# Modulation columns of the SSD part loaded at the head of each pair into the two large "ex" buffers

## The chip, the cores and the metric

The kernel runs on one core of one Trainium2 chip. The metric is device time in microseconds (us); lower is better. TensorE (PE), VectorE (DVE), ScalarE (ACT), GpSimd (POOL) and the queue of loads and stores (SP) each run their own list of instructions in order, and wait for one another by semaphores.

## The reference

One decoder layer at sequence 1024 and width 1024, all in float32. The part that the change touches is the modulation: six sections of 1024 numbers, each a sum over the 1024 inputs.

```python
c_act = jax.nn.silu(c)
mod = jnp.einsum('bd,de->be', c_act, w_ada[l]) + b_ada[l]
sh1, sc1, g1, sh2, sc2, g2 = [m[:, None, :] for m in jnp.split(mod, 6, axis=-1)]
h = x * (1.0 + sc1) + sh1
y = hybrid_mixer(h, ...)            # SSD scan (16 heads) + attention (16 heads), then W_out
x = layer_norm(ALPHA * x + (1.0 + g1) * y, ln1_g[l], ln1_b[l])
h = x * (1.0 + sc2) + sh2
ff = square(relu(h @ w_ff_in)) @ w_ff_out
x = layer_norm(ALPHA * x + (1.0 + g2) * ff, ln2_g[l], ln2_b[l])
```

The first section pair (`sh1`, `sc1`) is needed before anything else. The others are needed only after the mixer, so the kernel spreads them over it.

## The kernel before

The kernel goes through a start (h is made, eight tiles `h_hl` of 128 rows), eight SSD head pairs, attention, the output projection and the MLP. A float32 operand is split into a high part and a low remainder (`split`: the high part on POOL, ACT or DVE, the remainder always by a DVE subtraction, line 85), and each product is three matmuls.

`w_ada` is laid out as 48 columns of 512 KB, `raw_ada`, 128 x 1024 numbers each. For most of them `ada_sum` loads the column (on SP), POOL multiplies it by `c_act` (line 132), and DVE reduces it to 128 x 128, `ada_red` (line 134). PE then sums over the partitions (`adar_ps`) and DVE adds the bias (`mod_t`, line 202). `ada_red` has four buffers (`bufs=4`).

`w_prep` loads 512 KB of a projection weight, `raw_w`, and splits it in two halves `w_hl` of 128 x 512. `raw_w` and the 14 `raw_ada` of the SSD part share one tag, "raw", with two buffers: a load of either waits until the last reader of the buffer's older content is done (the subtraction of a `w_hl`, or the reduction of a column).

The SSD pairs run in this loop; `ssd(p)` makes the decays (`ea` and `scores` on ACT, from rows that are read back from DRAM) and the state, `conv_tile` and `z_tile` make the projections of the next pair, and `ada_some(2)` starts two columns and ends the two of the pair before:

```python
for p in range(NPAIR - 1):
    wn = w_prep(w_in[XI + p + 1])[0]
    ssd(p, *xz[p])
    xz.append((conv_tile(p + 1, "qk", "qk", wn), z_tile(p + 1)))
    ...
    ada_some(2)
```

The tag "ex" has two buffers of 8 KB per partition. In the kernel before it is first used in attention, by `w2_sums`. What stands where on each engine is decided by a scheduler that lays the whole program out beforehand; the code above gives it the order in which things are asked for, and it may move an instruction ahead of others that its model holds to be late.

Of the kernel before, what the change touches and what calls it, by code (L numbers as in the profile page):

```python
# [32 lines left out]
def layer_kernel(ctx, tc, x, xT, cols, rows3, w_ada, b_ada, w_in, w_dtf, w_out, ln_rows, w1, w2, out):  # L33
    nc = tc.nc

    def tap(name, t):
        if TAPS is not None and name in TAPS:
            shape = list(t.shape)
            o = nc.dram_tensor(f"tap_{name}", shape, F32, kind="ExternalOutput").ap()
            nc.sync.dma_start(out=o, in_=t)  # L40
# [9 lines left out]
    def T4(tag, name, dt=F32, shape=(P, 1024)):  # L50
        return sb.tile(list(shape), dt, name=name, tag=tag, bufs=SLOTS[tag])

    def R4(tag, name, shape=(P, 1024)):
        return T4(tag, name, F32R, shape)
# [3 lines left out]
    def PT(tag, name, shape=(P, 512), dt=F32):  # L58
        return ps.tile(list(shape), dt, name=name, tag=tag, bufs=PB[tag])

    def mm(o, l, r, start, stop):
        nc.tensor.matmul(o, l, r, start=start, stop=stop)  # L62

    def load(o, i):
        return nc.sync.dma_start(out=o, in_=i)
# [29 lines left out]
    ones = cst.tile([P, P], F32, name="ones")  # L95
# [29 lines left out]
    SH1, SC1, G1, SH2, SC2, G2 = range(6)  # L125
    mod_t = cst.tile([P, 6, KT], F32, name="mod_t")

    def ada_sum(sec, j, tag, name):

        raw = T4(tag, "raw_ada", shape=(P, KT, P))  # L130
        load(raw, w_ada[sec * 8 + j])
        nc.gpsimd.tensor_tensor(raw, raw, c_act.unsqueeze(2).broadcast_to([P, KT, P]), op=ALU.mult)  # L132
        red = sb.tile([P, P], F32, name="ada_red", tag="q2", bufs=4)
        nc.vector.tensor_reduce(red, raw.rearrange("p k c -> p c k"), axis=mybir.AxisListType.X, op=ALU.add)  # L134
        return red
# [4 lines left out]
    ADA_TAGS = ["P"] * 5 + ["pt"] * 4 + ["cum"] * 2 + ["P"] * 5  # L140
# [4 lines left out]
    def h_tile(j):  # L145
        pst = PT("t", "ada_ps", (P, 2))
        for i, sec in enumerate((SC1, SH1)):
            if j < PE_ADA:
                raw = T4(ADA_TAGS[2 * j + i], "raw_ada", shape=(P, KT, P))
                load(raw, w_ada[sec * 8 + j])  # L150
                for k in range(KT):
                    mm(pst[:, i:i + 1], raw[:, k, :], c_act[:, k:k + 1], k == 0, k == KT - 1)
            else:
                mm(pst[:, i:i + 1], ada_sum(sec, j, ADA_TAGS[2 * j + i], "r"), ones[:, 0:1], True, True)
        nc.vector.scalar_tensor_tensor(mod_t[:, SC1, j:j + 1], pst[:, 0:1], 1.0, b_t[:, 8 + j:9 + j],
                                       op0=ALU.add, op1=ALU.add)
        nc.vector.tensor_tensor(mod_t[:, SH1, j:j + 1], pst[:, 1:2], b_t[:, j:j + 1], op=ALU.add)
        xt = T4("v", "xt")
        marks["xt"] = load(xt, xT[j * P:(j + 1) * P, :])
        nc.scalar.activation(xt, xt, AF.Identity, scale=mod_t[:, SC1, j:j + 1], bias=mod_t[:, SH1, j:j + 1])  # L160
        t = sb.tile([P, 2, T], F32R, name="h_hl", tag="hx", bufs=SLOTS["hx"])
        split(xt, t[:, 0, :], t[:, 1, :], "dve" if j >= HI_DVE else "act")
        hT.append((t[:, 0, :], t[:, 1, :]))
# [22 lines left out]
    g_rows = {}  # L186
    gsum = {}

    def ada_rest(sec, j):
        red = ada_sum(sec, j, "raw", "r")  # L190
        yield
        pst = PT("mm", "adar_ps", (P, P))
        if sec in (G1, G2):
            mm(pst, ones, red, True, True)
            if j == 0:
                gsum[sec] = dr.tile([P, 1024], F32, name=f"grow{sec}")
            g = sb.tile([P, P], F32, name="ada_g", tag="q2", bufs=4)
            nc.vector.tensor_copy(g, pst)
            load(gsum[sec][:, j * P:(j + 1) * P], g)
        else:  # L200
            mm(pst[:, 0:1], red, ones[:, 0:1], True, True)
            nc.vector.tensor_tensor(mod_t[:, sec, j:j + 1], pst[:, 0:1], b_t[:, sec * 8 + j:sec * 8 + j + 1], op=ALU.add)

    rest = [(s, j) for s in (SC2, SH2, G2, G1) for j in range(8)]

    pend = []

    def ada_some(n):
        for g in pend:
            next(g, None)  # L210
        pend.clear()
        for _ in range(min(n, len(rest))):
            g = ada_rest(*rest.pop(0))
            next(g)
            pend.append(g)


    def w_prep(src, hi_eng="pool", tag="w"):

        raw = T4("raw", "raw_w", shape=(P, KT, P))  # L220
        ld = load(raw, src)
        w = []
        for kh in range(2):
            t = R4(tag, "w_hl", (P, 2, 4, P))
            split(raw[:, kh * 4:kh * 4 + 4, :], t[:, 0], t[:, 1], hi_eng)
            w.append(t)
        return w, ld
# [4 lines left out]
    def proj(w, half, M=P, o=None, tag="mm", ks=range(KT)):  # L232
# [8 lines left out]
        return o  # L241

    h_tile(0)


# [6 lines left out]
    for j in range(1, KT):  # L252
        h_tile(j)
# [97 lines left out]
    def z_tile(i):  # L351
        w, _ = w_prep(w_in[ZI + i])
        z = T4("qk", "z_s")
        for half in range(2):
            o = proj(w, half, tag="t")
            nc.scalar.activation(z[:, half * 512:half * 512 + 512], o, AF.Silu)
        return z
# [24 lines left out]
    def ssd(p, xs, z):  # L382
        g = p // 4
        h0 = 2 * p
        xp = PT("S", "s2_ps", (P, 8, P))
        for b in range(8):
            nc.tensor.transpose(xp[:, b, :], xs[:, b * P:(b + 1) * P], identf)
        xc = T4("qk", "xc", shape=(P, 8, 2, 64))
        xd = T4("qk", "xd", shape=(P, 8, 2, 64))
        nc.vector.tensor_tensor(xc, xp.rearrange("p c (h d) -> p c h d", h=2),  # L390
                                dtn[:, :, h0:h0 + 2].unsqueeze(3).broadcast_to([P, 8, 2, 64]), op=ALU.mult)
        nc.gpsimd.tensor_tensor(xd, xc, dte[:, :, h0:h0 + 2].unsqueeze(3).broadcast_to([P, 8, 2, 64]), op=ALU.mult)

        stp = PT("S", "s2_ps", (P, 8, P))
        for b in range(7):
            mm(stp[:, b, :], BN[g][:, b, :], xd[:, b, :, :].rearrange("p h d -> p (h d)"), True, True)
        pv = T4("pt", "prev", shape=(P, 8, P))
        nc.vector.memset(pv[:, 0, :], 0.0)
        for b in range(7):
            for h in range(2):  # L400
                hs = slice(h * 64, h * 64 + 64)
                nc.vector.scalar_tensor_tensor(pv[:, b + 1, hs], pv[:, b, hs], etot[:, b, h0 + h:h0 + h + 1],
                                               stp[:, b, hs], op0=ALU.mult, op1=ALU.add)

        ea = T4("misc", "ea")
        for h in range(2):
            load(ea[h * 64:h * 64 + 64, :], rowd[h0 + h:h0 + h + 1, :].broadcast_to([64, T]))
        nc.scalar.activation(ea, ea, AF.Exp)

        ydg = PT("S", "s2_ps", (P, 8, P))  # L410
        scs = []
        for h in range(2):
            ar = T4("cum", "arow", shape=(P, 8, P))
            load(ar.rearrange("p c l -> p (c l)"), rowd[h0 + h:h0 + h + 1, :].broadcast_to([P, T]))
            sc = T4("v", "scores", shape=(P, 8, P))
            for b in range(8):
                nc.scalar.activation(sc[:, b, :], ar[:, b, :], AF.Relu, bias=cs[:, b, h0 + h:h0 + h + 1], scale=-1.0)  # L417
            nc.scalar.activation(sc, sc, AF.Exp, scale=-1.0)
            nc.vector.tensor_tensor(sc, sc, CBM[g], op=ALU.mult)
            scs.append(sc)  # L420
        for b in range(8):
            for h in range(2):
                mm(ydg[h * 64:h * 64 + 64, b, :], xc[:, b, h, :], scs[h][:, b, :], True, True)
        yo = PT("S", "s2_ps", (P, 8, P))
        for b in range(8):
            mm(yo[:, b, :], pv[:, b, :], CT[g][:, b * P:(b + 1) * P], True, True)
        nc.vector.tensor_tensor(ea, yo.rearrange("p c d -> p (c d)"), ea, op=ALU.mult)
        nc.vector.tensor_tensor(ea, ydg.rearrange("p c d -> p (c d)"), ea, op=ALU.add)
        nc.vector.scalar_tensor_tensor(ea, xs, dsk[:, p:p + 1], ea, op0=ALU.mult, op1=ALU.add)
        if p == 0:  # L430
            tap("ssdy0", ea)
        nc.vector.tensor_tensor(ea, ea, z, op=ALU.mult)
        store(yd[p], ea)
# [5 lines left out]
    xz = [(conv_tile(0, "qk", "qk", w_x), z_tile(0))]  # L439
    for p in range(NPAIR - 1):  # L440
        wn = w_prep(w_in[XI + p + 1])[0]
        ssd(p, *xz[p])
        xz.append((conv_tile(p + 1, "qk", "qk", wn), z_tile(p + 1)))
        if p == FR_AT:
            forget_rows()
        if p == 1:
            group_prep(1)
        ada_some(2)
# [798 lines left out]
```

## Time and profile before

| | |
|---|---|
| median of 3 runs | 1739.49 us (1738.86 to 1745.34) |
| profiled execution, its own time | 1744.44 us |
| its span, first to last instruction | 1742.7 us |
| PE busy | 1654.0 us, 95% |
| DVE busy | 1229.9 us, 71% |
| POOL busy | 821.6 us, 47% |
| ACT busy | 747.2 us, 43% |
| mean granted TensorE clock | 0.980 of full speed |

The span is divided by the program itself: the start is 0 to about 65 us, the SSD pairs reach to about 365 us, and the rest is attention, the output projection and the MLP. An engine is counted as busy while an instruction runs on it; "idle before" is the time in which it stood, and the name behind the arrow is what it waited for. TensorE's clock has two levels, 1.2 and 2.4 GHz, told here as a granted clock of 0.5 and 1.0 of full speed.

### The profile page before, as it was taken

What the parts mean: (1) busy time and instruction counts of PE and PEld (TensorE: products, weight loads), DVE (VectorE), ACT (ScalarE), POOL (GpSimd) and SP (SyncE); (2) the same over time, 40 slices, a digit from 0 to 9 for tenths busy, and PEclk for the clock granted to TensorE, in tenths of its full rate; (3) what the DMA queues carried; (4) which work ended last, traced back from release to release, by engine and by line L of the source; (5) the groups of instructions that cost most, each with busy time, mean ns of one, the idle gap of its engine ahead of it and who ended that gap; (6) DMA issues with size and microseconds to landing.
All of it is one profiled execution on the core that took longest, in us unless ns stands there. A gap on an engine that the chain in (4) does not pass through costs nothing.

```text
span 1742.7 us, 22932 instructions
## 1 busy us (share of the span) xinstructions
PE 1654.0 (95%) x8316; PEld 1368.7 (79%) x8316; DVE 1229.9 (71%) x1898; ACT 747.2 (43%) x1321; POOL 821.6 (47%) x670
## 2 busy tenths in 40 slices
PE   8989899899999999999899999799999999999996
PEld 6777787788877878888778887688888878888885
DVE  7755777686777777676665379986767855646668
ACT  3458355414444444444565334633332334343322
POOL 5121332256566466454442345566656624704535
PEclk9999999999999999999999999899999999999998
DMA  8134343334444534434324644043444596676512
GB/s 331 37 123 147 109 145 109 121 130 151 161 142 170 169 134 167 137 121 132 119 97 130 221 157 169 37 175 133 146 143 160 172 340 212 247 242 205 194 36 96
DMA packets 112032, 268.72 MB, mean 154 GB/s; under 512 B 10128, under 2 KB 37008, under 8 KB 111920
## 3 DMA queue, kind: packets, MB, share of 16 engines
q1 hardware_dynamic: 111920, 267.27, 44.2%
q8 instruction: 65, 1.06, 0.3%
q14 instruction: 47, 0.39, 0.1%
HBM read 194.22 MB, written 64.62 MB: 149 GB/s over the span
## 4 chain that ended last, share of the span: by engine, by line
PE 60%; DVE 15%; DMA 8%; ACT 7%; POOL 5%; issue 4%; SPq 0%; DVEq 0%; ACTq 0%; POOLq 0%
PE mm_ps L62 18%; PE f_ps L957 15%; PE s_ps L1073 9%; PE y_ps L1073 7%; PE s_ps L62 5%; PE o_ps L62 4%; DVE ada_red L134 3%; PE t_ps L546 3%; DMA w_b<-in_w_dram 2%; ACT scores L417 2%; POOL w_b L182 2%; DMA raw_ada<-in_w_ada_dram 1%; DVE w_hl L85 1%; DVE conv_a L346 1%; DVE h_hl L85 1%
## 5 line engine op out<-in xcount | busy, mean ns | idle before, releaser
L62 PE MATMUL mm_ps<-h_hl,w_hl 128*128 128x512 f32 x2016 | 504.5, 400 | 10.9 <-POOL w_hl L79 6.1
L62 PEld LDWEIGHTS mm_ps<-h_hl,w_hl 128*128 128x128 f32 x2016 | 373.5, 191 | 88.3 <-POOL w_hl L79 6.9
L85 DVE TENSOR_TENSOR w_op<-raw_w,w_op 128x512 fp32r<-128x512 f32 (+1 forms) x149 | 186.9, 1260 | 23.2 <-ACT w_op L81 22.6
L957 PE MATMUL f_ps<-h_s,w_op 128*128 128x512 f32 x768 | 183.8, 394 | 6.4 <-ACT h_s L81 3.3
L957 PEld LDWEIGHTS f_ps<-h_s,w_op 128*128 128x128 f32 x768 | 146.0, 190 | 38.4 <-ACT h_s L81 3.7
L524 POOL TENSOR_SCALAR probs<-probs,m 128x128 f32<-128x128 f32 (+7 forms) x128 | 104.5, 822 | 127.3 <-DVE m L523 122.8
L81 ACT CAST w_op<-raw_w 128x512 fp32r<-128x512 f32 (+1 forms) x149 | 114.5, 774 | 100.2 <-PE f_ps L957 53.0
L1073 PE MATMUL s_ps<-w_op,a_op 128*128 128x512 f32 x672 | 153.7, 390 | 1.5 <-DVE a_op L85 1.1
L1073 PEld LDWEIGHTS s_ps<-w_op,a_op 128*128 128x128 f32 x672 | 125.9, 188 | 28.8 <-DVE a_op L85 1.6
L79 POOL TENSOR_SCALAR w_hl<-raw_w 128x512 fp32r<-128x512 f32 x86 | 60.5, 705 | 180.0 <-PE mm_ps L62 126.1
L85 DVE TENSOR_TENSOR a_op<-a_ld,a_op 128x1024 fp32r<-128x1024 f32 x53 | 75.5, 1427 | 98.4 <-ACT a_op L81 98.4
L132 POOL TENSOR_TENSOR raw_ada<-raw_ada,c_act 128x1024 f32<-128x1024 f32 x44 | 88.8, 2027 | 117.1 <-DMA raw_ada<-in_w_ada_dram 99.8
L522 ACT ACTIVATE probs<-probs,m 128x128 f32<-128x128 f32 (+7 forms) x128 | 99.1, 775 | 96.8 <-DVE m L521 86.5
L957 PE MATMUL f_ps<-h_hl,w_op 128*128 128x512 f32 x576 | 136.9, 389 | 0.0
L85 DVE TENSOR_TENSOR w_hl<-raw_w,w_hl 128x512 fp32r<-128x512 f32 x88 | 81.5, 929 | 68.5 <-POOL w_hl L79 68.2
L548 ACT CAST pt_hl<-t_ps 128x512 fp32r<-128x512 f32 (+1 forms) x160 | 84.8, 542 | 100.7 <-PE t_ps L546 97.3
L957 PEld LDWEIGHTS f_ps<-h_hl,w_op 128*128 128x128 f32 x576 | 108.0, 188 | 22.4
L81 ACT CAST a_op<-a_ld 128x1024 fp32r<-128x1024 f32 x53 | 55.7, 1054 | 159.7 <-PE s_ps L1073 80.7
L62 PE MATMUL o_ps<-pt_hl,v_s 128*128 128x256 f32 (+1 forms) x640 | 110.9, 300 | 8.7 <-DVE pt_hl L549 5.4
L549 DVE TENSOR_TENSOR pt_hl<-t_ps,pt_hl 128x512 fp32r<-128x512 f32 (+1 forms) x160 | 99.6, 630 | 23.1 <-ACT pt_hl L548 21.6
L519 DVE CUSTOM_DVE_ANT_0 probs<-s_ps,cumrow 128x128 f32<-128x128 f32 (+7 forms) x128 | 94.8, 750 | 28.9 <-PE s_ps L62 20.1
L1073 PE MATMUL y_ps<-w_op,a_op 128*128 128x512 f32 x504 | 114.7, 389 | 0.0
(254 smaller groups left out, 3136.1 us busy)
## 6 DMA issues: line engine op xcount, KB each, us to landing
raw_w<-in_w_dram SPq DMA_DIRECT2D x57, 512.0 KB, 4.3
a_ld<-ad SPq DMA_DIRECT2D x49, 512.0 KB, 4.4
raw_ada<-in_w_ada_dram SPq DMA_DIRECT2D x48, 512.0 KB, 3.6
raw_w<-in_w_in_dram SPq DMA_DIRECT2D x44, 512.0 KB, 3.7
w_b<-in_w_dram SPq DMA_DIRECT2D x14, 1024.0 KB, 8.0
w2t<-w_b SPq DMA_DIRECT2D x14, 1024.0 KB, 4.3
ad<-a_s SPq DMA_DIRECT2D x28, 512.0 KB, 3.4
raw_w<-w2t SPq DMA_DIRECT2D x28, 512.0 KB, 4.8
```

What stands on the lines that cost most here:

```text
L62: nc.tensor.matmul(o, l, r, start=start, stop=stop)
L79: nc.gpsimd.tensor_scalar(hi, raw, 1.0, 1.0, op0=ALU.mult, op1=ALU.mult)
L81: nc.scalar.copy(hi, raw)
L85: eng.tensor_tensor(lo, raw, hi.bitcast(F32), op=ALU.subtract)
L132: nc.gpsimd.tensor_tensor(raw, raw, c_act.unsqueeze(2).broadcast_to([P, KT, P]), op=ALU.mult)
L519: nc.vector.tensor_tensor_reduce(out=pt, in0=sp[:, :W], in1=cum[:, :W], op0=ALU.add, op1=ALU.max, scale=1.0, scalar=-3.0e38, accum_out=m[: ...
L522: nc.scalar.activation(pt, pt, AF.Exp, bias=m[:, 1:2], scale=1.0, accum_out=m[:, 2:3])
L524: nc.gpsimd.tensor_scalar(pt, pt, m[:, 3:4], 1.0, op0=ALU.mult, op1=ALU.mult)
L548: nc.scalar.copy(hl[:, 0, :n], tp[:, :n])
L549: nc.vector.tensor_tensor(hl[:, 1, :n], tp[:, :n], hl[:, 0, :n].bitcast(F32), op=ALU.subtract)
L957: nc.tensor.matmul(o, l, r, start=first and k == 0 and m == 0, stop=last and k == 3 and m == 2, skip_group_check=True)
L1073: nc.tensor.matmul(banks[j], ahl[a_][:, n, js], whl[w_][:, n, :], start=first and d == 0 and n == 0 and m == 0, stop=last and d == ND - 1 ...
```

## The change

The load of a column is taken out of `ada_sum` into `ada_raw`. At the head of each of the seven pairs of the loop, `ada_load(2)` asks for the loads of the two columns that `ada_some(2)` sums at the pair's end, and they go to "ex" in place of "raw". These are 14 columns: 8 of section SC2 and 6 of SH2. Later columns, in attention, still use "raw". No sum is added or left out.

```diff
+    def ada_raw(sec, j, tag):
         raw = T4(tag, "raw_ada", shape=(P, KT, P))
         load(raw, w_ada[sec * 8 + j])
+        return raw
+
+    def ada_sum(sec, j, tag, raw=None):
+
+        if raw is None:
+            raw = ada_raw(sec, j, tag)
         nc.gpsimd.tensor_tensor(raw, raw, c_act.unsqueeze(2).broadcast_to([P, KT, P]), op=ALU.mult)
...
-    def ada_rest(sec, j):
-        red = ada_sum(sec, j, "raw", "r")
+    def ada_rest(sec, j, raw):
+        red = ada_sum(sec, j, "raw", raw)
         yield
...
+    loaded = []
+
+    def ada_load(n):
+        for _ in range(n):
+            loaded.append((*rest[len(loaded)], ada_raw(*rest[len(loaded)], "ex")))
...
-            g = ada_rest(*rest.pop(0))
+            at = rest.pop(0)
+            g = ada_rest(*at, loaded.pop(0)[2] if loaded else None)
...
         wn = w_prep(w_in[XI + p + 1])[0]
+        ada_load(2)
         ssd(p, *xz[p])
```

From line 128 on, a line of the changed kernel has a number that is higher by 5 (132 and 134 become 137 and 139), behind line 189 by 11 (392 becomes 403).

The scheduler lays out the two programs differently up to the end of the SSD pairs; from there on every engine has the same rows. Three places follow. The numbers behind the names tell buffers apart.

SP at the start, the loads behind the first projection weights, in the kernel before (`raw_w_635` and `raw_w_696` are weights, `raw_ada_946` and `951` the first two columns of the SSD part):

```order
L65 DMA raw_w_567<-in_w_in_dram 128x1024
L65 DMA raw_w_635<-in_w_in_dram 128x1024
L65 DMA raw_w_696<-in_w_in_dram 128x1024
L65 DMA raw_w_862<-in_w_in_dram 128x1024
L65 DMA raw_ada_946<-in_w_ada_dram 128x1024
L65 DMA raw_ada_951<-in_w_ada_dram 128x1024
L65 DMA rowd_403<-rows_404 16x1024
```

The same place in the changed kernel, whose first two columns (`raw_ada_704` and `706`) already stand some eight loads earlier, among those of the h tiles:

```order
L65 DMA raw_w_567<-in_w_in_dram 128x1024
L65 DMA raw_w_635<-in_w_in_dram 128x1024
L65 DMA raw_ada_964<-in_w_ada_dram 128x1024
L65 DMA raw_ada_966<-in_w_ada_dram 128x1024
L65 DMA raw_ada_1365<-in_w_ada_dram 128x1024
L65 DMA raw_ada_1367<-in_w_ada_dram 128x1024
L65 DMA raw_w_696<-in_w_in_dram 128x1024
L65 DMA raw_w_866<-in_w_in_dram 128x1024
```

The columns of the first three pairs have moved into the start, six loads in all, and stand ahead of weights and of the store of the decay rows.

DVE at the start, the last h tiles, in the kernel before (`h_hl_256`, `277` and `298` are h tiles 5, 6 and 7, counted from 0):

```order
L85 TENSOR_TENSOR h_hl_256<-xt_253,h_hl_256 128x1024
L155 SCALAR_TENSOR_TENSOR mod_t_96<-ada_ps_259,col_92 128x1
L157 TENSOR_TENSOR mod_t_96<-ada_ps_259,col_92 128x1
L85 TENSOR_TENSOR w_hl_569<-raw_w_567,w_hl_569 128x512
L83 CAST h_hl_277<-xt_274 128x1024
L155 SCALAR_TENSOR_TENSOR mod_t_96<-ada_ps_280,col_92 128x1
L157 TENSOR_TENSOR mod_t_96<-ada_ps_280,col_92 128x1
L85 TENSOR_TENSOR h_hl_277<-xt_274,h_hl_277 128x1024
L83 CAST h_hl_298<-xt_295 128x1024
L85 TENSOR_TENSOR h_hl_298<-xt_295,h_hl_298 128x1024
L262 COPY dtf_raw_303<-mm_ps_304 32x512
```

And in the changed kernel:

```order
L85 TENSOR_TENSOR h_hl_256<-xt_253,h_hl_256 128x1024
L139 TENSOR_REDUCE ada_red_951<-raw_ada_704 128x128
L160 SCALAR_TENSOR_TENSOR mod_t_96<-ada_ps_259,col_92 128x1
L162 TENSOR_TENSOR mod_t_96<-ada_ps_259,col_92 128x1
L139 TENSOR_REDUCE ada_red_954<-raw_ada_706 128x128
L160 SCALAR_TENSOR_TENSOR mod_t_96<-ada_ps_280,col_92 128x1
L162 TENSOR_TENSOR mod_t_96<-ada_ps_280,col_92 128x1
L85 TENSOR_TENSOR w_hl_569<-raw_w_567,w_hl_569 128x512
L83 CAST h_hl_277<-xt_274 128x1024
L85 TENSOR_TENSOR h_hl_277<-xt_274,h_hl_277 128x1024
L83 CAST h_hl_298<-xt_295 128x1024
L85 TENSOR_TENSOR h_hl_298<-xt_295,h_hl_298 128x1024
```

Two reductions now stand ahead of h tiles 6 and 7, and two more (of columns 964 and 966) directly behind these rows and ahead of the copies of `dtf_raw`.

POOL at the end of pair 1 in the kernel before (`w_hl_1253` and `1256` are the two halves of one weight; `raw_ada_1347` and `1352` the columns of that pair):

```order
L79 TENSOR_SCALAR w_hl_1253<-raw_w_1251 128x512
L132 TENSOR_TENSOR raw_ada_1347<-raw_ada_1347,c_act_94 128x1024
L132 TENSOR_TENSOR raw_ada_1352<-raw_ada_1352,c_act_94 128x1024
L79 TENSOR_SCALAR w_hl_1256<-raw_w_1251 128x512
L79 TENSOR_SCALAR w_hl_1359<-raw_w_1357 128x512
L79 TENSOR_SCALAR w_hl_1362<-raw_w_1357 128x512
```

And the same weights in the changed kernel (`1257` and `1260` are the halves of that weight):

```order
L79 TENSOR_SCALAR w_hl_1257<-raw_w_1255 128x512
L79 TENSOR_SCALAR w_hl_1260<-raw_w_1255 128x512
L79 TENSOR_SCALAR w_hl_1359<-raw_w_1357 128x512
L79 TENSOR_SCALAR w_hl_1362<-raw_w_1357 128x512
L79 TENSOR_SCALAR w_hl_1529<-raw_w_1527 128x512
L137 TENSOR_TENSOR raw_ada_1608<-raw_ada_1608,c_act_94 128x1024
L137 TENSOR_TENSOR raw_ada_1610<-raw_ada_1610,c_act_94 128x1024
```

No multiplication stands between the two halves any more, since this pair's columns are summed at the start.

## Rows read from the trace of the kernel before

**Rows 1.** Busy time of each engine by stage: pairs 0-1, pair 1, all behind the SSD part

```profile
core 0: us, PE busy (x) PEld busy (x) DVE busy (x) ACT busy (x) POOL busy (x), PEclk, DMA share, GB/s
...
107.00:150.00 43.00, 39.37 (x210) 31.71 (x209) 23.01 (x34) 42.70 (x79) 4.66 (x7) 0.96 0.43 152
150.00:190.00 40.00, 33.37 (x174) 26.62 (x173) 25.00 (x34) 19.91 (x33) 10.65 (x8) 0.91 0.46 147
...
390.00:1742.00 1352.00, 1299.96 (x6441) 1078.92 (x6439) 956.94 (x1512) 567.05 (x1033) 700.76 (x570) 0.98 0.46 158
```

**Rows 2.** Waits of PE from 50 to 365 us: total, times, longest

```profile
PE mm_ps L62 <- POOL w_hl L79: 6.1, 2, 5.1
...
PE s_ps L387 <- DVE ea L427: 1.8, 1, 1.8
...
PE mm_ps L62 <- DVE rows L315: 0.3, 1, 0.3
```

**Rows 3.** Timeline of DVE from 14 to 66 us: start, duration, line, operation, idle before

```profile
22.17 2.19 DVE L85 TENSOR_TENSOR h_hl<-xt,h_hl 128x1024 fp32r<-128x1024 f32 x1 [0.23 <-ACT h_hl L81]
...
47.49 1.98 DVE L134 TENSOR_REDUCE ada_red<-raw_ada 128x128 f32<-128x1024 f32 x1
...
57.41 1.23 DVE L85 TENSOR_TENSOR h_hl<-xt,h_hl 128x1024 fp32r<-128x1024 f32 x1
62.14 1.28 DVE L262 COPY dtf_raw<-mm_ps 32x512 f32<-32x512 f32 x2 [3.50 <-PE mm_ps L62]
```

**Rows 4.** Timeline of PE from 50 to 104 us

```profile
79.80 2.05 PE L62 MATMUL s_ps<-conv_a 128*128 128x128 f32 x16 [1.97 <-ACT conv_a L348]
...
98.17 1.04 PE L314 MATMUL r_ps<-identf,cs 128*16 128x128 f32 x8 [2.43 <-DVE cs L300]
```

**Rows 5.** Timeline of POOL from 160 to 198 us

```profile
172.76 2.93 POOL L132 TENSOR_TENSOR raw_ada<-raw_ada,c_act 128x1024 f32<-128x1024 f32 x1 [7.11 <-DMA raw_ada<-in_w_ada_dram]
181.46 1.90 POOL L132 TENSOR_TENSOR raw_ada<-raw_ada,c_act 128x1024 f32<-128x1024 f32 x1 [5.78 <-DMA raw_ada<-in_w_ada_dram]
183.32 0.62 POOL L79 TENSOR_SCALAR w_hl<-raw_w 128x512 fp32r<-128x512 f32 x1
```

**Rows 6.** Timeline of PE from 160 to 200 us

```profile
163.10 15.78 PE L62 MATMUL mm_ps<-h_hl,w_hl 128*128 128x512 f32 x67
183.99 1.22 PE L62 MATMUL mm_ps<-h_hl,w_hl 128*128 128x512 f32 x2 [5.12 <-POOL w_hl L79]
185.96 9.33 PE L62 MATMUL mm_ps<-h_hl,w_hl 128*128 128x512 f32 x34 [0.75 <-DVE w_hl L85]
```

**Rows 7.** Timeline of ACT from 160 to 200 us

```profile
187.78 1.28 ACT L408 ACT_TABLE_LOAD   x1 [10.65 <-DMA ea<-rowd]
...
192.60 1.06 ACT L348 ACTIVATE conv_a<-conv_a 128x1024 f32<-128x1024 f32 x1
```

**Rows 8.** Timeline of SP, loads and stores as issued, 160 to 198 us

```profile
180.61 0.33 SPq L65 DMA_DIRECT2D yd<-ea  x1
183.24 1.09 SPq L65 DMA_DIRECT2D ea<-rowd  x2
```

**Rows 9.** Timeline of DVE from 160 to 200 us

```profile
179.36 1.22 DVE L432 TENSOR_TENSOR ea<-ea,z_s 128x1024 f32<-128x1024 f32 x1
```

**Rows 10.** Timeline of POOL from 294 to 336 us

```profile
300.16 2.22 POOL L132 TENSOR_TENSOR raw_ada<-raw_ada,c_act 128x1024 f32<-128x1024 f32 x1 [10.38 <-DMA raw_ada<-in_w_ada_dram]
```

**Rows 11.** Timeline of ACT from 294 to 336 us

```profile
310.43 1.06 ACT L408 ACTIVATE ea<-ea 128x1024 f32<-128x1024 f32 x1 [9.14 <-DVE conv_a L346]
```

**Rows 12.** Timeline of PE from 294 to 336 us

```profile
304.31 1.83 PE L62 MATMUL s_ps<-xd,b_nat 128*128 128x128 f32 x14 [1.37 <-POOL xd L392]
...
315.86 2.02 PE L62 MATMUL s_ps<-conv_a,prev 128*128 128x128 f32 x16 [1.26 <-DVE prev L402]
...
329.31 0.59 PE L62 MATMUL adar_ps<-ones,ada_red 128*128 128x1 f32 x2 [2.21 <-DVE mod_t L202]
```

**Rows 13.** Loads by kind: KB each, median us from issue to landing

```profile
raw_ada<-in_w_ada_dram SPq DMA_DIRECT2D x48, 512.0 KB, 3.6
```

More of the change, by code (lines that the diff above doesn't have):

```diff
@@ L126, in layer_kernel @@
     mod_t = cst.tile([P, 6, KT], F32, name="mod_t")
-    def ada_sum(sec, j, tag, name):
+    def ada_raw(sec, j, tag):
         raw = T4(tag, "raw_ada", shape=(P, KT, P))
         load(raw, w_ada[sec * 8 + j])
+        return raw
+    def ada_sum(sec, j, tag, raw=None):
+        if raw is None:
+            raw = ada_raw(sec, j, tag)
         nc.gpsimd.tensor_tensor(raw, raw, c_act.unsqueeze(2).broadcast_to([P, KT, P]), op=ALU.mult)
@@ L153, in h_tile @@
             else:
-                mm(pst[:, i:i + 1], ada_sum(sec, j, ADA_TAGS[2 * j + i], "r"), ones[:, 0:1], True, True)
+                mm(pst[:, i:i + 1], ada_sum(sec, j, ADA_TAGS[2 * j + i]), ones[:, 0:1], True, True)
         nc.vector.scalar_tensor_tensor(mod_t[:, SC1, j:j + 1], pst[:, 0:1], 1.0, b_t[:, 8 + j:9 + j],
```

## The prediction, as put on record before the run

> **What bounds the kernel now.** I read the page first: PE is busy for 95% of the span, so only the idle 5%, and stretches of low clock, can be won. Then I set the rows of both programs side by side, engine by engine: they differ up to the end of the SSD pairs and are equal behind it. The stages show how little that leaves. Behind 390 us PE works 1299.96 of 1352 us in both kernels [rows 1]; nothing there can change but by its start. From 50 to 365 us PE has 14 kinds of waits, 26.0 us in all, of which 6.1 are waits for a weight's high part [rows 2]. Those 26 us, and the low clock behind some of them, are all that the change can touch on the good side. The forecast is the shift with which PE reaches the end of the SSD pairs.
>
> The largest wait is at the end of pair 1, and the change aims at it. POOL has two column multiplications in its list between the halves of one weight; the second waits 5.78 us for its load, ends at 183.36, and only then comes the half that PE needs [rows 5]. PE stands for 5.12 us, then 0.75 for the low part, and does 36 matmuls until 195.3 [rows 6]. The 67 matmuls ahead took 15.78 us, 0.236 each; 36 would take 8.5, and the 1.22 + 9.33 us of these are 2.1 more. The granted clock of that stage is 0.91 against 0.96 in the stage before [rows 1]: PE fell to 1.2 GHz in the gap. So the gap cost 5.12 + 0.75 + 2.1 = 8.0 us.
>
> **What the change does.** It does not do what its code says: the scheduler does not leave the loads at the head of each pair. The columns of the first three pairs go into the start, in loads, multiplications and reductions. The rest stand near where they stood, but no longer share a buffer with weights.
>
> *The start.* The sum of a column is a POOL multiplication of 1.90 us [rows 5] and a DVE reduction of 1.98 [rows 3]. DVE is nearly without gaps from 14 to 58.6 us, and it makes the h tiles that PE waits for. Two reductions now stand ahead of tiles 6 and 7: 2 x 1.98 = 4.0 us. I take 3.0 of it through to PE, since PE reached the products of tile 7 about a microsecond after its parts were ready: they end at 58.64, and DVE then waits 3.50 us for PE [rows 3]. Two more reductions stand ahead of the copies of `dtf_raw`. DVE's 3.50 us of slack there cover 3.96 of them nearly, but they follow loads that wait for the first two reductions to free "ex" (3.6 us of load [rows 13], 1.90 of multiplication, 1.98 of reduction), so I take 1.5 more: 4.5 in all. The bounds are 1 (tile 6 was not late) and 4 x 1.98 = 7.9 (all of it).
>
> *The port.* A DVE subtraction of an h tile took 1.23 us alone and 2.19 while POOL multiplied [rows 3], so a multiplication beside it costs up to 1.0. A POOL multiplication took 2.93 and 1.90 us [rows 5]; the long one stood beside DVE products. Two of the moved multiplications stand among those of the last h tiles: I take +1.0, bounds 0 and 4 (one subtraction for each of the first four). The Trainium skill ("SBUF — State Buffer", section "Who interferes with whom") says that a DVE instruction with two inputs in SBUF contends with a GpSimd instruction that reads SBUF, the first to start holding the port for its whole length, and that a reduction never contends. The trace agrees on both: 2.19 against 1.23 for the subtraction, 1.98 for the reduction. By that rule taken for all four, the sum would be 3 us higher.
>
> *Given back in pair 0.* The reductions that stood ahead of `cs` in DVE's list are gone. PE waited 2.43 us for it [rows 4]; a reduction and a half weight less gives about 1.6 of it. Between 107 and 150 us ACT is busy 42.70 of 43 us [rows 1], so this stretch neither absorbs nor returns anything: what PE and ACT are late at its start, they are late at its end. Shift there: 4.5 + 1.0 - 1.6 = +3.9.
>
> *The end of pair 1.* POOL no longer waits there, so the 8.0 us go. But ACT is late next. It stands 10.65 us for `ea` and ends the SiLU of `conv_a` at 193.66 [rows 7], and the transposes that PE does at 195.3 need it. The load of `ea` was issued at 183.24, behind the store at 180.61 [rows 8] that waits for DVE's last product, which ended at 180.58 [rows 9]. The reduction ahead of that product is gone, 2.0 us; the SiLU would come at about 191.1 with 0.5 more from DVE. PE without the gap would be there at 178.88 + 8.5 = 187.4 and wait 3.8 us. The gain is 195.3 - 191.1 = 4.2, and a wait of 3.8 is again one at which the clock falls, 2.0 by the measure above. I take -2.2; bounds 0 and -8.0.
>
> *Pairs 2 to 6.* PE's wait of 1.8 us for `ea`, at 265 us, stood behind a reduction: -1.8 [rows 2]. Near 300 us POOL waits 10.38 us for a column [rows 10]; behind it stand `xd` and weights, and ACT 9.14 us for a convolution [rows 11]. PE waits 1.37, 1.26 and 2.21 us [rows 12]. With own buffers the weight is not queued behind a column's reduction and ACT is some 5 us earlier; 1.37 and 1.26 go. The wait of 2.21 for `mod_t` remains in part, since the scheduler's row of `mod_t` still stands behind the products of `scores`: 1.3 of it goes. Together -3.9; bounds -1 and -8 (the low clock as well).
>
> *The sum:* +4.5 + 1.0 - 1.6 - 2.2 - 1.8 - 3.9 = -4.0 us. On the profiled execution (1744.44) this gives 1740.4; that execution is 5 us above the median of the runs, so on the median it is **1735.5 us**.
>
> **The rivals.** *Faster:* ACT does not take over the gap. The store and `ea` are then ahead of PE, all 8.0 us go, and near 300 us all 8: 5.5 - 1.6 - 8.0 - 1.8 - 8 = -13.9, 1725.6 us. For it speaks that DVE loses its reductions throughout; against it that `ea` is loaded behind a store in SP's list in both programs, and the load itself takes time whatever POOL does.
>
> *Slower:* the start is dearer. POOL's list there has the multiplication of a third pair's column ahead of the second half of `w_hl_569`'s weight, and that column can only be loaded when an "ex" buffer is free: reduction, load, multiplication, 1.98 + 3.6 + 1.90 = 7.5 us in series on POOL, in front of what PE does next. If PE runs out of the first half before that, the start costs 4 x 1.98 + 4 + the rest of the chain, some 15 us, with a fall of the clock. The sum is then 15 - 1.6 - 2.2 - 1.8 - 3.9 = +5.5, 1745 us; it turns slower than before once the start costs over 9.5, and slower by over 0.5% from about 18. For it: the list is in order and DVE has no slack before 58 us. Against it: in PE's list of the changed kernel 19 matmuls of the first half now stand together, and other products before them, to fill that time.
>
> *No effect:* since the loads are not at the heads of the pairs, later columns land no earlier and each term is near its small bound: +2 - 1 - 2 = -1, 1738 us. Nearly the same on the clock as my forecast, and told apart only by the wait at 184 us.
>
> **How the numbers follow.** A measurement here tells about 0.5%, 8.7 us, from no change. Forecast, with its own range of -10 to +3: 0.45. Faster rival: 0.22. Slower rival: 0.22, about half of it beyond 8.7. No effect: 0.11. Of the forecast some 0.05 lies beyond -8.7. So faster 0.27, within 0.5% 0.61, slower 0.12. The range takes in both rivals and leaves the tails: -15 to +9, 1724 to 1748.
>
> **What would show it.** Right: DVE reaches the copies of `dtf_raw` some 4 us later; PE arrives at 107 us of before 3 to 4 us late; no wait for a weight near 184 us, but one for `conv_a` or `ea` a few us long there; the stage behind the SSD part unchanged. Wrong: PE waits over 2 us for a weight between 65 and 80 us; a new wait for `mod_t` or for "ex" buffers that the first six sums hold; the gap at 184 us gone without one in its place.

## The result, and the profile after

The change made the kernel slower: median 1754.8 us (1749.17 to 1756.19) against 1739.49 (1738.86 to 1745.34), five runs of each, ratio 1.0068 with a 95% interval of 1.0052 to 1.0085, which is +9 to +15 us (the medians are 15.3 us apart, the means 12.2). The prediction had 1735.5 us in a range of 1724 to 1748. Here and below, medians and ratios leave out a few executions of 2.7 to 9.3 ms.

The two profiled executions are only 4.8 us apart in span (1742.7 and 1747.5), so the loss has to be read by place. I took the start of PE's n-th matmul in each program (there are 8316 in both) and subtracted. The time in the head of the table is that of the kernel before. Where the two programs order their matmuls differently, the n-th is not the same product, so single entries inside the SSD part are good to a microsecond or two.

| lag of PE, us, at n = | 200 (57 us) | 300 (80) | 600 (147) | 700 (163) | 800 (193) | 900 (212) | 1400 (298) | 1800 (374, end of the SSD part) |
|---|---|---|---|---|---|---|---|---|
| after | +6.7 | +11.2 | +11.3 | +11.0 | +2.8 | +9.9 | +12.4 | +11.0 |

Nearly all of the loss is made by 80 us. At the end of pair 1 the change wins 8.2 us, as it should, and 7.1 of them are lost at once. Behind the SSD part the lag stays (11.5 at 505 us) and then falls to 5.7 by 776 us, in work that both kernels do alike. The windows of 400 to 900 us, first of the kernel before, then of the changed one, show what that is (the column behind POOL's is the granted clock):

```profile
400.00:900.00 500.00, 478.03 (x2750) 400.94 (x2749) 366.21 (x847) 241.11 (x523) 276.10 (x295) 0.98 0.42 144
```

```profile
400.00:900.00 500.00, 478.59 (x2770) 399.92 (x2769) 368.79 (x853) 240.38 (x523) 278.40 (x298) 1.00 0.43 146
```

The profiled execution of the kernel before was granted 0.98 there, and at 1744.44 us it was longer than most of that kernel's runs; that of the changed kernel, with 1.00, was the shortest of its five. Ten of the twelve other runs below catch up 2.4 to 4.8 us on that execution of the kernel before in the same stretch (505 to 776 us), so it is that execution which was slow there. I take the 11.0 us at the end of the SSD part as the effect, and they lie in the measured interval.

**The start.** The timeline of PE after the change, to be held against [rows 4]:

```profile
61.06 0.65 PE L62 MATMUL mm_ps<-h_hl,dtf_hl 128*32 128x512 f32 x2 [1.84 <-DVE h_hl L83]
...
64.04 1.35 PE L62 MATMUL mm_ps<-h_hl,dtf_hl 128*32 128x512 f32 x4 [1.87 <-DVE h_hl L85]
65.19 2.33 PE L62 MATMUL b_ps<-h_hl,w_hl 128*128 128x512 f32 x5
67.33 1.70 PE L62 MATMUL c_ps<-h_hl,w_hl 128*128 128x512 f32 x5
...
73.12 0.43 PE L276 MATMUL t_ps<-identf,dtf_raw 32*128 32x32 f32 x4
...
91.52 3.33 PE L62 MATMUL s_ps<-conv_a 128*128 128x128 f32 x16 [1.64 <-ACT conv_a L359]
```

The same place in the kernel before:

```profile
62.40 1.32 PE L62 MATMUL b_ps<-h_hl,w_hl 128*128 128x512 f32 x5
63.56 1.31 PE L62 MATMUL c_ps<-h_hl,w_hl 128*128 128x512 f32 x5
64.80 0.43 PE L265 MATMUL t_ps<-identf,dtf_raw 32*128 32x32 f32 x4
```

PE waits for both parts of h tile 6, and ten products behind them take 2.33 + 1.70 us in place of 1.32 + 1.31; the granted clock from 64 to 69 us is 0.66, where it is 1.00 in the kernel before. At the transposes of `dtf_raw` PE is 8.3 us late. The last row was at 79.80, so 3.4 us more are lost up to there, and its 16 small products take 3.33 us in place of 2.05. DVE of the changed kernel, and behind it POOL, show why the tile is late:

```profile
37.48 2.64 DVE L85 TENSOR_TENSOR h_hl<-xt,h_hl 128x1024 fp32r<-128x1024 f32 x1
...
45.48 2.92 DVE L85 TENSOR_TENSOR h_hl<-xt,h_hl 128x1024 fp32r<-128x1024 f32 x1
...
55.69 1.97 DVE L139 TENSOR_REDUCE ada_red<-raw_ada 128x128 f32<-128x1024 f32 x1
...
57.71 1.96 DVE L139 TENSOR_REDUCE ada_red<-raw_ada 128x128 f32<-128x1024 f32 x1
...
61.04 2.95 DVE L85 TENSOR_TENSOR h_hl<-xt,h_hl 128x1024 fp32r<-128x1024 f32 x1
63.91 2.38 DVE L83 CAST h_hl<-xt 128x1024 fp32r<-128x1024 f32 x1
66.33 1.22 DVE L85 TENSOR_TENSOR h_hl<-xt,h_hl 128x1024 fp32r<-128x1024 f32 x1
67.47 3.86 DVE L139 TENSOR_REDUCE ada_red<-raw_ada 128x128 f32<-128x1024 f32 x2
71.24 1.27 DVE L273 COPY dtf_raw<-mm_ps 32x512 f32<-32x512 f32 x2
75.38 0.69 DVE L85 TENSOR_TENSOR w_hl<-raw_w,w_hl 128x512 fp32r<-128x512 f32 x1 [2.88 <-POOL w_hl L79]
75.99 2.92 DVE L357 SCALAR_TENSOR_TENSOR conv_a<-conv_u,col,conv_a 128x1023 f32<-128x1023 f32 x1
```

```profile
61.01 1.90 POOL L137 TENSOR_TENSOR raw_ada<-raw_ada,c_act 128x1024 f32<-128x1024 f32 x1 [10.27 <-DVE h_hl L83]
63.26 2.48 POOL L137 TENSOR_TENSOR raw_ada<-raw_ada,c_act 128x1024 f32<-128x1024 f32 x1 [0.35 <-DMA raw_ada<-in_w_ada_dram]
72.87 1.90 POOL L137 TENSOR_TENSOR raw_ada<-raw_ada,c_act 128x1024 f32<-128x1024 f32 x1 [7.12 <-DMA raw_ada<-in_w_ada_dram]
74.73 0.62 POOL L79 TENSOR_SCALAR w_hl<-raw_w 128x512 fp32r<-128x512 f32 x1
```

DVE of the kernel before, the same three subtractions, the cast, and the first tap of the convolution:

```profile
37.26 1.22 DVE L85 TENSOR_TENSOR h_hl<-xt,h_hl 128x1024 fp32r<-128x1024 f32 x1
...
46.36 1.21 DVE L85 TENSOR_TENSOR h_hl<-xt,h_hl 128x1024 fp32r<-128x1024 f32 x1
...
55.29 1.21 DVE L85 TENSOR_TENSOR h_hl<-xt,h_hl 128x1024 fp32r<-128x1024 f32 x1
56.68 0.69 DVE L83 CAST h_hl<-xt 128x1024 fp32r<-128x1024 f32 x1 [0.18 <-ACT xt L160]
...
66.28 1.28 DVE L346 SCALAR_TENSOR_TENSOR conv_a<-conv_u,col,conv_a 128x1023 f32<-128x1023 f32 x1
```

DVE comes to the copies of `dtf_raw` at 71.24 in place of 62.14 [rows 3], 9.1 us late, where some 4 had been set as the sign of being right. Four reductions stand ahead of them (7.8 us). The subtractions of h tiles 3, 4 and 6 took 2.64, 2.92 and 2.95 us in place of 1.21 to 1.22, and the cast of tile 7 took 2.38 in place of 0.69: 6.6 us more. (Two other subtractions in the start became 2.2 us shorter.) Each of the four runs beside a multiplication: that of 61.04 begins 0.03 us behind POOL's, and 2.95 is nearly 1.90 and 1.21 one after the other. By the low part of tile 5, ahead of all moved reductions, PE was already 2.7 us late (55.82 in place of 53.15).

The second two reductions, at 67.47, fill the slack that DVE had ahead of the copies. The copies end at 72.51, and PE comes to the transposes at 73.12, directly from its last product: it did not wait for them. What follows them is late by another road: POOL's multiplication of 72.87, for the third pair, stands ahead of a half weight, so DVE stands 2.88 us for it, and a tap of the convolution took 2.92 us beside the next multiplication, where it took 1.28. PE then stands for `conv_a`.

Only four reductions have moved. Those of the third pair's columns, multiplied at 72.87 and 75.80, come at 200.64 and 204.82, behind PE's first sums over the partitions (`adar_ps`) at 200.15 and 204.28: `ada_red` has four buffers.

**The end of pair 1.** PE, then ACT, then SP after the change, to be held against [rows 6], [rows 7] and [rows 8]:

```profile
174.10 23.98 PE L62 MATMUL mm_ps<-h_hl,w_hl 128*128 128x512 f32 x103
200.15 0.38 PE L62 MATMUL adar_ps<-ones,ada_red 128*128 128x1 f32 x2 [2.07 <-ACT conv_a L354]
202.51 1.97 PE L381 MATMUL s_ps<-identf,conv_a 128*128 128x128 f32 x8 [1.99 <-ACT conv_a L359]
```

```profile
196.59 1.28 ACT L419 ACT_TABLE_LOAD   x1 [8.46 <-DMA ea<-rowd]
...
201.40 1.06 ACT L359 ACTIVATE conv_a<-conv_a 128x1024 f32<-128x1024 f32 x1
```

```profile
189.44 0.32 SPq L65 DMA_DIRECT2D yd<-ea  x1
192.05 1.09 SPq L65 DMA_DIRECT2D ea<-rowd  x2
```

The 103 matmuls now run without a wait for a weight. Then PE stands twice, for copies and a SiLU that ACT does late, since it stood 8.46 us at an exponential whose rows were loaded behind a store.

**Near 330 us** the wait for `mod_t`, 2.21 us in [rows 12], has grown (line 202 of the kernel before is 207 here; up to line 206 the numbers are higher by 5, not 11):

```profile
340.34 0.59 PE L62 MATMUL adar_ps<-ones,ada_red 128*128 128x1 f32 x2 [4.03 <-DVE mod_t L207]
```

### The profile page after: what moved, and what is told of

It reads as the page before. It is cut to its first block, busy times and chain, and to the rows that moved or that the text cites. A ratio compares the mean times of both kernels' runs of the same rounds, so it can differ in the third digit from the quotient of the medians.

```text
span 1747.5 us, 22940 instructions
## 1 busy us (share of the span) xinstructions
PE 1650.6 (94%) x8316; PEld 1363.9 (78%) x8316; DVE 1237.2 (71%) x1898; ACT 749.5 (43%) x1323; POOL 823.5 (47%) x670
## 4 chain that ended last, share of the span: by engine, by line
PE 58%; DVE 13%; ACT 8%; DMA 5%; POOL 5%; issue 4%; SPq 0%; DVEq 0%; ACTq 0%; POOLq 0%
PE mm_ps L62 17%; PE f_ps L969 15%; PE s_ps L1085 9%; PE y_ps L1085 7%; PE s_ps L62 5%; PE o_ps L62 3%; PE t_ps L558 2%; ACT scores L428 2%; POOL w_b L187 2%; DMA w_b<-in_w_dram 1%; DVE probs L531 1%; DMA y_raw<-yd 1%; DVE w_hl L85 1%; DVE ada_red L139 1%; DMA raw_w<-in_w_dram 1%
## 5 line engine op out<-in xcount | busy, mean ns | idle before, releaser
L85 DVE TENSOR_TENSOR w_hl<-raw_w,w_hl 128x512 fp32r<-128x512 f32 x88 | 77.9, 891 | 72.9 <-POOL w_hl L79 72.6
```

The lines of the kernel that those rows point to most:

```text
L85: eng.tensor_tensor(lo, raw, hi.bitcast(F32), op=ALU.subtract)
```

## The experiments

Theory A was that the six sums moved into the start make the loss; theory B, that it sits in the later stages. Theory C was that at the end of pair 1 ACT's `ea` takes the gain away; rival D, that something else would. Each ratio below is against runs of the kernel before taken together with that run (medians 1741.7 to 1743.7 us). The lags of all runs, read in the same way against the same execution of the kernel before:

| lag of PE, us | 57 us | 80 | 147 | 163 | 193 | 212 | 298 | 374 |
|---|---|---|---|---|---|---|---|---|
| e1_held | -0.4 | +3.3 | +8.7 | +7.7 | +1.6 | +7.4 | +8.6 | +7.2 |
| e2_first_three | +8.4 | +13.1 | +11.8 | +11.9 | +3.3 | +10.0 | +9.7 | +10.1 |
| e3_last_four | +4.7 | +4.7 | +4.4 | +5.0 | +6.6 | +6.6 | +8.1 | +6.2 |
| e4_short_reductions | +3.9 | +5.2 | +3.4 | +4.0 | -4.6 | +3.4 | +12.5 | +2.6 |
| e5_no_multiplications | +7.4 | +8.9 | +11.2 | +10.2 | +1.6 | +7.5 | +6.9 | +6.9 |
| e6_loads_only | +2.4 | +2.3 | +1.4 | +1.9 | -6.7 | -0.3 | +8.3 | -1.5 |
| e7_asked_late | +7.3 | +12.3 | +11.9 | +12.4 | +3.9 | +10.5 | +13.0 | +11.9 |
| e8_late_loads | -0.4 | -0.4 | +11.0 | +10.9 | +1.4 | +3.1 | +5.0 | -7.2 |
| e11_ea_later | +7.2 | +11.6 | +11.6 | +12.2 | +4.1 | +4.2 | +6.3 | +6.5 |
| e12_late_loads_ea_later | -0.6 | -0.6 | +11.6 | +11.5 | +2.0 | +3.4 | +3.5 | -7.5 |
| e13_before_ea_later | 0.0 | 0.0 | +0.8 | +0.5 | +1.2 | +1.2 | +1.7 | +2.7 |
| e14_from_pair_1 | -0.3 | -0.4 | +5.6 | +5.5 | -4.0 | -2.1 | -2.1 | -13.1 |

### What in the start costs the time

**e4_short_reductions**, the reductions of the first six columns cut to an eighth:

```diff
-        nc.vector.tensor_reduce(red, raw.rearrange("p k c -> p c k"), axis=mybir.AxisListType.X, op=ALU.add)
+        of = raw[:, 0:1, :] if sec == SC2 and j < 6 else raw
+        nc.vector.tensor_reduce(red, of.rearrange("p k c -> p c k"), axis=mybir.AxisListType.X, op=ALU.add)
```

> As changed, but DVE reduces only one of eight blocks of the first six columns (seven eighths of those sums are left out), so that DVE's time for them nearly goes while POOL's multiplications stay. If the reductions' own time (six of 1.97 us, four of them ahead of the copies of dtf_raw) makes the loss, PE's lag at the products behind the first SiLU falls from 11.7 to about 3 us; if POOL's multiplications beside DVE's subtractions make it, it stays at 7 or more.

**e5_no_multiplications**, the multiplications of the same columns left out:

```diff
-        nc.gpsimd.tensor_tensor(raw, raw, c_act.unsqueeze(2).broadcast_to([P, KT, P]), op=ALU.mult)
+        if not (sec == SC2 and j < 6):
+            nc.gpsimd.tensor_tensor(raw, raw, c_act.unsqueeze(2).broadcast_to([P, KT, P]), op=ALU.mult)
```

> As changed, but the first six columns are not multiplied by c_act (that part is left out), so that POOL's time for them goes while the reductions stay. If the slowed subtractions and the weights queued behind the multiplications make the loss, PE's lag there falls from 11.7 to about 4 us; if the reductions' own time makes it, it stays at 8 or more.

**e6_loads_only** has both edits. All three leave parts of the sums out, so they stand for a time and not for a result, and each ran once (1743.93, 1749.48 and 1738.81 us); they are read by the lag:

> As changed, but of the first six columns neither the multiplication is done nor more than one of eight blocks reduced (those sums are left out); the six early loads remain. If the loads or the order of the queue cost nothing in the start, PE's lag at the products behind the first SiLU is 0 to 2 us (11.7 as changed, 5.2 with short reductions, 8.9 without multiplications); if the loads themselves hold up the start, it stays at 4 or more.

Of the 11.2 us at 80 us (11.7 at the row of 79.80) the short reductions leave 5.2, the missing multiplications 8.9, both together 2.3. By these differences the reductions are worth 6.0 (with the multiplications in place) to 6.6 (without), the multiplications 2.3 to 2.9. e4's 5.2 lies between the two limits that had been set, e5's 8.9 in the branch of the reductions, e6's 2.3 just above its first branch. But the multiplications' share is a lower bound. DVE of e6_loads_only:

```profile
45.85 2.84 DVE L85 TENSOR_TENSOR h_hl<-xt,h_hl 128x1024 fp32r<-128x1024 f32 x1
```

This is the subtraction of h tile 4 that took 1.21 us before. No early column is multiplied here; the new order has put it beside a multiplication of the start's own columns (POOL has three of them from 41.55 to 47.61). That is 1.6 of the 2.3 us that remain, so little is left for the loads. e5 has the same (2.85), and there the scheduler also put the two reductions one place further ahead, so the split is good to about a microsecond. What e4 and e6 lose between 212 and 298 us stands in layouts of their own (e6 waits 3.97 us for `ea` there) and is not followed here.

**e3_last_four** loads early for pairs 3 to 6 only:

```diff
-        ada_load(2)
+        if p >= 3:
+            ada_load(2)
```

> Only the columns of pairs 3 to 6 go to the large buffers; the first three pairs are as before. The scheduler moves pair 3's two columns into the start. Theory A: two early sums cost what two reductions and two multiplications cost, about 4 to 6 us at 64 us, and the rest of the start's loss is absent; the gap at the end of pair 1 stays; behind the SSD part 3 to 6 us late, 1742 to 1746 us. Rival (a fixed cost of using the buffers early): 10 us late as in the change.

It came out at 1746.73 us, ratio 1.0031 (1.0020 to 1.0042), just above what A gave, with a lag of 4.7 us at 57 and 5.0 at 163 us. The size came out, but not for the reason given. The two early columns are loaded and multiplied in the start; DVE does their reductions only at 231.48 and 238.66. So no reduction moved, and loads and multiplications alone made the 4.7 us: the subtractions of h tiles 3 and 4 took 2.83 and 2.92 us beside multiplications, 3.3 us more than before, and 0.6 us of lag is there by 30 us. The scheduler here moved the loads and multiplications of pair 3's columns, which POOL multiplies at 225 and 232 us in the kernel before, as far forward as those of pair 0 in the changed kernel: a free buffer was enough. **e2_first_three** has the opposite condition, `if p < 3`:

> Only pairs 0 to 2 load early into the large buffers; the columns of pairs 3 to 6 share buffers with the weights as before the change. Theory A: the start is that of the changed kernel, PE is 11 us late at the end of the SSD part, 1749 to 1756 us. Theory B: most of the loss goes, 1740 to 1745 us.

1748.76 us, ratio 1.0033 (1.0018 to 1.0048). The lag follows the changed kernel to the end of the SSD part (10.1), as theory A says; the measured time is a little under what it gave.

### The place in the code

**e7_asked_late** asks for the loads at the end of the pair:

```diff
-        ada_load(2)
         ssd(p, *xz[p])
...
+        ada_load(2)
         ada_some(2)
```

> Own buffers, but asked for at the end of each pair in the code, right ahead of the sums. If it is the free buffers and not the place in the code that lets the scheduler move six sums into the start, the time is that of the changed kernel, 1748 to 1756 us, with the same lag of 11 us; if the place at the head of the pair matters, it is near the kernel before.

1753.84 us, ratio 1.0076 (1.0057 to 1.0094), the lags of the changed kernel within 1.5 us. Every engine has the rows of the changed kernel in the same order, so the 1.5 us also show how far two executions of one order differ by place. The place at the head of the pair is not what does it; the free buffers are.

**e1_held** queues the loads behind the pair's weight:

```diff
-        wn = w_prep(w_in[XI + p + 1])[0]
-        ada_load(2)
+        wn, wl = w_prep(w_in[XI + p + 1])
+        with after(wl):
+            ada_load(2)
```

> The loads keep to the head of their pair: each pair's two column loads are queued behind that pair's weight load, so none can move into the start; buffers as in the change. Theory A (the loss is the six sums that moved into the start): PE reaches the products behind the first SiLU at about 80 us as before the change, the 11 us are gone, and the time is at or a few us below the kernel before, 1733 to 1740 us. Theory B (the loss sits in the later stages, where the columns in own buffers upset the order of ea, conv_a and mod_t): still 1748 to 1756 us.

A miss for theory A: 1751.09 us, ratio 1.0040 (1.0026 to 1.0053), a time in theory B's range. The start is back (-0.4 at 57 us), but 9.1 us are lost between 57 and 147 us. POOL's two multiplications, from 69.88 on, took 5.62 us, and DVE does both reductions (77.25 to 81.01) between the taps of the convolutions and the chain to `cs`; two taps beside the multiplications took 4.11 us in place of 2.47. PE of e1_held waits for a weight and for `cs`:

```profile
83.66 7.02 PE L62 MATMUL mm_ps<-h_hl,w_hl 128*128 128x512 f32 x20 [3.81 <-DVE w_hl L85]
...
102.57 1.88 PE L325 MATMUL r_ps<-identf,cs 128*16 128x128 f32 x8 [2.87 <-DVE cs L311]
```

So DVE has no room before 107 us either. That it is again the sums, and theory A only too narrow on the stretch, is read from these rows; e14 below bears it out for pair 0.

### Where the gain at the end of pair 1 went

**e11_ea_later** is the changed kernel with one instruction of ACT moved; the rows of all other engines are the same:

```diff
-        nc.scalar.activation(a, a, AF.Silu)
+        marks[f"conv{i}"] = nc.scalar.activation(a, a, AF.Silu)
...
-        nc.scalar.activation(ea, ea, AF.Exp)
+        if p == 4:
+            with after(marks["conv11"]):
+                nc.scalar.activation(ea, ea, AF.Exp)
+        else:
+            nc.scalar.activation(ea, ea, AF.Exp)
```

> As changed, and one exponential of ACT (the ea of pair 4, whose load waits for a store) is queued behind the SiLU of group 1's second convolution in place of ahead of its first; every other engine's rows are those of the changed kernel. Theory C (at the end of pair 1 the freed 8 us are lost again because ACT stands at this ea ahead of conv_a): PE's two waits there (2.07 and 1.99 us) and the low clock behind them go, the lag behind the SSD part falls from 11.0 to 4 to 6 us, 1743 to 1750 us. Rival D (PE is caught by the next thing, weights or the bias sum): the lag stays at 9 to 11 us.

1747.54 us, ratio 1.0026 (1.0011 to 1.0040). From 193 to 212 us the lag rose by 7.1 us in the changed kernel and by 0.1 here; at the end of the SSD part it is 6.5, a little over theory C's 4 to 6. PE of e11_ea_later passes the place without a wait but for 0.24 us:

```profile
191.40 8.00 PE L62 MATMUL mm_ps<-h_hl,w_hl 128*128 128x512 f32 x34 [0.24 <-DVE w_hl L85]
199.25 0.28 PE L62 MATMUL adar_ps<-ones,ada_red 128*128 128x1 f32 x2
199.38 1.07 PE L381 MATMUL s_ps<-identf,conv_a 128*128 128x128 f32 x8
```

Theory C holds, rival D falls. **e13_before_ea_later** has the same edit on the kernel before:

> The kernel before, with only ACT's exponential of pair 4 (ea) moved behind the SiLU of group 1's second convolution. If the end of pair 1 has two causes in series (POOL's multiplication first, ACT's ea behind it), the POOL gap of 5 us stays and the lag behind the SSD part is 0, within 1.5 us: no measurable change. If ea alone was worth the 7 us that it gave on top of the change, it is 4 to 7 us faster.

1742.1 us, ratio 1.0001 (0.9990 to 1.0012): nothing, and POOL's gap is still there (4.99 us at 184.05). The lag of 2.7 at 374 us is more than the 1.5 that had been allowed, with no place to which I can put it. The gap has two causes in series. From 163 to 212 us, taking POOL's alone gives 1 us (the change), ACT's alone 0 (e13), both 8 (e11).

### A version that beats both

**e8_late_loads** keeps the large buffers, but queues each pair's loads behind the weight of `z`:

```diff
-        w, _ = w_prep(w_in[ZI + i])
+        w, marks["z"] = w_prep(w_in[ZI + i])
...
-        ada_load(2)
         ssd(p, *xz[p])
...
+        with after(marks["z"]):
+            ada_load(2)
         ada_some(2)
```

> The same as the run beside it without the move of ea on ACT. Theory C: 4 to 6 us slower than that run, since ACT takes over the gap; rival D: the same time.

**e12_late_loads_ea_later** adds the edit of e11:

> Columns in the large buffers, but asked for at the end of each pair and queued behind the weight load of z, so that none moves into the start; and pair 4's ea on ACT queued as in the run beside it. Theories A and C together: the start is that of the kernel before, pair 0 is late by up to 6 us since its sums still move ahead, the gap at the end of pair 1 goes with nothing in its place: lag 0 to -6 us, 1733 to 1741 us. Rival: pair 0 costs what it cost with held loads (8 us at 147 us) and the time stays at 1742 to 1748 us.

e8 took 1729.16 us, ratio 0.9921 (0.9903 to 0.9940), e12 1729.79, 0.9932 (0.9912 to 0.9952). Both beat the kernel before, and e12 adds nothing. By the letter of e8's expectation that speaks for rival D, but the pair is no test of it: in e8's layout ACT has the first SiLU of that place (193.93) ahead of `ea` (198.02) already, which the expectation had overlooked. e12 is faster than it was given, and for another reason: pairs 0 and 1 still lose 11 us by 147 us, more than the 6 that were allowed, and the stages behind win more.

**e14_from_pair_1** leaves pair 0 as it was (`if p >= 1` ahead of e8's `with`):

> Late asking behind the weight load of z, for pairs 1 to 6 only; pair 0's columns share buffers with weights as before the change. If the 11 us that late loads still lost by 147 us come from pair 0's sums (waits of 1.1 and 3.1 us at 88 and 92 us), the lag there falls to 2 to 5 us and the kernel is 4 to 7 us faster than with late loads for all: 1722 to 1727 us. If they come from pair 1's columns and ACT's order (waits for z_s of 3.6 and 4.4 us), the time stays at 1728 to 1731 us.

1725.78 us, ratio 0.9909 (0.9893 to 0.9924), in the range of the first branch, with a lag of 5.6 at 147 us, a little over what that branch gave. Pair 0 costs nothing any more (-0.6 at 105 us), and 6.2 us are lost up to 147 us, nearly all behind 127 us, where PE waits for `z_s`. Behind that the buffers of their own do what they were to do: the wait for `mod_t` near 330 us is 0.75 in this kernel, against 4.03 in the changed one. PE of e14_from_pair_1:

```profile
133.38 0.86 PE L325 MATMUL r_ps<-identf,cs 128*16 128x128 f32 x4 [3.58 <-ACT z_s L367]
138.82 0.81 PE L325 MATMUL r_ps<-identf,cs 128*16 128x128 f32 x3 [4.58 <-ACT z_s L367]
...
321.94 9.13 PE L62 MATMUL mm_ps<-h_hl,w_hl 128*128 128x512 f32 x39 [0.75 <-DVE mod_t L207]
```

The orders of e8, e12 and e14 differ from that of the kernel before far into the stages behind the SSD part (to about 980 us in e14), so not all of the rest of the gain is due to the SSD part: 13.1 us of lag are won by its end in e14, 7.2 in e8. What makes ACT late at 133 us was not tried.

## Why the prediction was wrong

**The bound.** That PE bounds the kernel, and that the rows behind the SSD part shift as one, held: 11.0 us at 374 us, 11.5 at 505. (PE's 14 kinds of waits from 50 to 365 us add up to 27.0 us, not to the 26.0 of the prediction.)

**The start: the step that failed.** The mechanism was named, column sums on DVE and POOL where DVE has no gaps. The size of the term failed: it was taken as +4.5 + 1.0, and PE is 8.3 us late at the transposes of `dtf_raw` and 11.2 at 80 us. Three parts of it were mis-sized.

The port, taken at +1.0 for the last h tiles, took 6.6 us of DVE's time, and it hit tiles 3 and 4 as well, which made PE 2.7 us late ahead of any moved reduction. How much of the 11.2 it is, the runs only bound: 2.3 to 2.9 as the lower bound of e4 to e6, and 4.7 where only the loads and multiplications of two columns came early (e3). The Trainium skill ("SBUF — State Buffer", section "Who interferes with whom") also names the cast among the instructions that can contend, when its operands meet conditions; the trace agrees, 2.38 us beside a multiplication against 0.69. The row of 1.98 that the prediction gave for a reduction [rows 3] stands beside no multiplication, but the reading holds: reductions beside a multiplication took 1.82 to 2.04 us in the kernel before.

"I take 3.0 of it through to PE" left out the clock. The reductions delay h tile 6 from the front, since its `mod_t` stands behind both; PE waited 1.84 and 1.87 us for its two parts, and the 10 matmuls behind them took 2.33 + 1.70 us at a granted clock of 0.66, 1.4 us more. The second two reductions, on the other hand, cost PE nothing at the copies: the slack of 3.50 us took them, as the prediction had it.

The stretch behind the copies was at nothing in the sum, and it made 3.4 us of the 11.7 at the row of 79.80. POOL's multiplications for the third pair stood there ahead of a half weight and beside DVE's taps; the prediction had them only in the slower rival. Between the same two places e4 and e5 lose 1.4 and 1.5 us, e6 nothing, so both the reductions and the multiplications take part. That the third pair's reductions also go into the start was a misreading (they come at 200.64 and 204.82).

**Given back in pair 0.** -1.6 was predicted, -1.7 came between 80 and 106 us. 1.5 were lost again by 163 us.

**The end of pair 1.** -2.2 predicted, -1.1 measured, of the same two parts, and with the wait for `conv_a` that had been named as a sign: 8.2 won (8.0 had been read from the gap), 7.1 lost to ACT, `ea` and the clock. e11 and e13 show this step by step. The faster rival fell on the point that was argued against it, the load of `ea` behind a store.

**Pairs 2 to 6.** -1.8 for the wait at 265 us was wrong: the wait for `ea` of 1.7 us is still there, and from 212 to 298 us the change lost 2.4. Of -3.9 near 300 us, -1.4 came. "ACT is some 5 us earlier" failed: ACT's `ea` there waits for DVE's state product, not for a weight, and starts 12.6 us behind [rows 11] with PE 12.4 late. So DVE gets its `scores` late, and `mod_t`, which stands behind them, keeps PE 4.03 us. ACT, then DVE, after the change:

```profile
323.07 1.06 ACT L419 ACTIVATE ea<-ea 128x1024 f32<-128x1024 f32 x1 [9.21 <-DVE prev L413]
```

```profile
337.86 1.22 DVE L430 TENSOR_TENSOR scores<-scores,cbm 128x1024 f32<-128x1024 f32 x1 [3.05 <-ACT scores L429]
339.00 1.22 DVE L438 TENSOR_TENSOR ea<-s_ps,ea 128x1024 f32<-128x1024 f32 x1
340.14 0.15 DVE L207 TENSOR_TENSOR mod_t<-adar_ps,col 128x1 f32<-128x1 f32 x1
```

**The rivals.** The slower one, "the start is dearer", came nearest: it gave 15 us for the start and +5.5 in all. The start came out at 11.2, under the 15, but the later stages gave back almost nothing (11.2 - 1.7 + 1.5 - 1.1 + 2.4 - 1.4 = 10.9), where the prediction set 9.5 us against it. POOL's chain of loads was part of it (72.87 for the third pair's multiplication), but it reached PE through DVE's list; PE did not run out of the first half there. "No effect" fell.

## What to carry to other kernels

Where a scheduler orders a program, giving a load buffers of its own also gives it leave to move the work behind that load; look in the new order for what it put in the most loaded stretch, and hold it back with an explicit edge (e8, e14; e1 shows that the edge must reach past the full stretch). Count moved work by the engine that is full in its new place, every instruction at its price beside the others, and follow it to the end of the stretch. Before a stall is booked as a gain, find what the next engine in line was waiting for in the same gap: here POOL's cause alone gave 1 us, ACT's none, and both together 8.

## What the runs showed of the hardware that was not expected

A DVE cast of 128 x 1024 from SBUF took 2.38 us beside a POOL multiplication and 0.69 alone, a subtraction 2.64 to 2.95 against 1.21, and a tap of the convolution 2.92 against 1.28, while reductions took 1.82 to 2.04 us beside one (kernel before) and 1.96 to 1.98 with POOL idle. Waits of under 2 us can be followed by a low clock: behind those of 1.84 and 1.87 us at 61 and 64 us the granted clock was 0.66 (64 to 69 us), and five matmuls took 2.33 us, where five took 1.30 to 1.32 at the higher level.
